# A transformer layer in float32r: weight chunks that begin at an offset of their own in each large product

## The chip, the cores and the metric

The kernel runs on one core of one Trainium2 chip. The metric is the device time of one execution in microseconds. TensorE (PE) multiplies, with its weight loads traced apart (PEld); VectorE (DVE) and ScalarE (ACT) do the elementwise work, GpSimd (POOL) and SyncE (SP) issue most transfers. SBUF, the on-chip memory, has 128 partitions; an address here is a byte within a partition, and "byte 96 of 128" means an address that leaves 96 when divided by 128.

## What is computed

One layer over 256 positions of width 2,048: a projection into two attention branches and their gates, the two attentions, a merge, an output projection, and a gated FFN with a short convolution (width 5,632). All weights are float32.

```python
h = rms_norm(x, norm_mix_pre)
c_q, c_kv, k_r, q_s, k_s, v_s, gates = split(h @ w_in)
...
merged = g[:, :, 0] * (o_a @ w_o_mla) + g[:, :, 1] * (o_b @ w_o_swa)
x = x + rms_norm(merged @ w_out, norm_mix_post)
h = rms_norm(x, norm_ffn_pre)
a, b = split(h @ ffn_w_up)
c = conv_b + sum(conv_w[j] * shifted(a, j) for j in range(3))
x = x + rms_norm((gelu(c) * b) @ ffn_w_down, norm_ffn_post)
```

## The kernel before

A float32 product is done as three float32r products. Each operand is split into a high part (its value rounded to float32r) and a low part (what is left), and `mm3` (lines 142 to 145) adds high x high, high x low and low x high into one PSUM accumulator. The activations are the stationary operand, 128 columns at a time, and lie split in SBUF slots (`ah`, `al`, `bh`, `bl`, and `gh`, `gl` for the FFN); the weights are the moving operand.

`wchunk` (lines 101 to 120) brings a chunk of weights: up to 1,024 float32 in each partition, as two row blocks of 512 columns or four of 256. The DMA lands it in a raw tile (3 buffers); ACT writes the high part `whi` by a casting copy (L118), DVE subtracts for the low part `wlo` (L119). The two go into the pool `ring`, which has 5 buffers of each. A chunk's buffers come free when the matmuls that read them are done, so the chain DMA, ACT, DVE, PE runs some chunks ahead of the matmuls.

`gemm` (lines 147 to 174) is one large product: all 16 to 24 row blocks of a weight matrix, 512 columns of it (320 or 256 in three cases), for both halves of the 256 positions. It calls `wchunk`, then `mm3` for each row block and half, so 96 to 144 matmuls. After each chunk `tick` runs what is due of the attention or the convolution, small matmuls and transposes that stand between those of the product. There are 58 calls of `gemm`. A few chunks aren't in the ring: the last `w_out` product has its first three, and the first FFN product its first four, in pools of their own (`own`). The projections inside the MLA attention call `wchunk` too, and there the chunk is in some matmuls the stationary operand (`qn`, `kn`, lines 610 to 612).

The order of work on the engines comes from the program's order and the tile framework's scheduler. Nothing in it depends on addresses.

Where things lie matters here. Two small tiles, `line_a` (96 bytes) and `line_b` (32 bytes), stand ahead of the activation slots. With them, the slots, the ring's `whi` and `wlo` and the attention's operands all begin at byte 96 of 128. The ring's chunks are 4,096 bytes, a row block of 512 columns 2,048 bytes and a stationary block 512, so in every matmul of a large product both operands begin at byte 96 of 128.

Of the kernel before, what the change touches and what calls it, by code (L numbers as in the profile page):

```python
# [12 lines left out]
F32R = mybir.dt.float32r  # L13
# [6 lines left out]
P = 128  # L20
# [21 lines left out]
def trunk_layer(ctx, tc, x, g_mix_pre, g_mix_post, g_ffn_pre, g_ffn_post, w_in, g_q, w_q, g_kv, w_kv,  # L42
# [13 lines left out]
    base = ctx.enter_context(tc.tile_pool(name="base", bufs=1))  # L56
    ring = ctx.enter_context(tc.tile_pool(name="ring", bufs=RING))

    def sb(pl, shape, name, dt=F32, tag=None, bufs=None):
        return pl.tile(shape, dt, name=name, tag=tag or name, **({"bufs": bufs} if bufs else {}))  # L60
# [10 lines left out]
    def warm_up(n):  # L71
        for i in range(n):
            tc.keep_in_program_order(pe.matmul(warm[:, 0:P], ident_b, ident_b, start=True, stop=True))

    warm_up(WARM[0])
    causal = sb(base, [P, P], "causal", BF16)
# [20 lines left out]


    cnt = [0]

    def wchunk(src, shape, own=None, rawp=None):
        i = cnt[0]
        cnt[0] += 1
        n = int(np.prod(shape))
        raw = rawp.tile([P, 1024], F32, name=f"raw{i}", tag="xraw") if rawp else \
            ring.tile([P, 1024], F32, name=f"raw{i}", tag="raw", bufs=RAW)
        dst = raw[:, :n]
        if len(shape) == 2:
            dst = dst.rearrange("p (a b) -> p a b", a=shape[0])
        elif len(shape) == 3:  # L110
            dst = dst.rearrange("p (a b c) -> p a b c", a=shape[0], b=shape[1])
        if len(shape) == 3:
            for k in range(shape[0]):
                nc.sync.dma_start(dst[:, k], src[:, k])
        else:
            nc.sync.dma_start(dst, src)
        hi, lo = ((own or ring).tile([P, 1024], F32R, name=f"w{part}{i}", tag="w" + part) for part in ("hi", "lo"))
        act.copy(hi[:, :n], raw[:, :n])  # L118
        vec.tensor_tensor(lo[:, :n], raw[:, :n], hi[:, :n].bitcast(F32), op=ALU.subtract)  # L119
        return hi, lo  # L120
# [8 lines left out]
    def tick():  # L129
        for f in steps.pop(now[0], ()):  # L130
            f()
        now[0] += 1
# [5 lines left out]
    def new_acc(tag):  # L138
        i = cnt[0]
        return [pacc.tile([P, 512], F32, name=f"acc{tag}_{i}_{t}", tag="acc") for t in range(NT)]  # L140

    def mm3(o, ah, al, bh, bl, start, stop):
        pe.matmul(o, ah, bh, start=start, stop=False)  # L143
        pe.matmul(o, ah, bl, start=False, stop=False)  # L144
        pe.matmul(o, al, bh, start=False, stop=stop)  # L145

    def gemm(xh, xl, w, k0, nk, c0, n, split=False, pre=None, extra=None):

        kc = 1024 // n if n in (256, 512) else 2
        acc = new_acc("g")  # L150
        todo = []
        cuts = [0, 1, 2] + list(range(4, nk + 1, 2)) if pre else list(range(0, nk, kc)) + [nk]
        for ci, (k, ke) in enumerate(zip(cuts[:-1], cuts[1:])):
            kk = ke - k
            src = w[(k0 + k) * P:(k0 + k + kk) * P, c0:c0 + n].rearrange("(a p) n -> p a n", p=P)
            if pre and ci == 0:
                pre(k, ke)
            hi, lo = wchunk(src, [kk, n], *(extra or {}).get(ci, ()))
            if pre and ke < nk:
                pre(ke, cuts[ci + 2])  # L160
            for j in range(kk):
                kt = k + j
                wh, wl = hi[:, j * n:(j + 1) * n], lo[:, j * n:(j + 1) * n]
                for t in range(NT):
                    def go(kt=kt, t=t, wh=wh, wl=wl):
                        mm3(acc[t][:, :n], xh(k0 + kt)[:, t * P:(t + 1) * P],
                            xl(k0 + kt)[:, t * P:(t + 1) * P], wh, wl, kt == 0, kt == nk - 1)
                    if split and t == 1:
                        todo.append(go)
                    else:  # L170
                        go()
            tick()
        return acc, todo
# [59 lines left out]
    def columns(dst, rows, n):  # L233
        pg = pss.tile([P, 512], F32, name=f"pg{rows.tensor.name}", tag="s")
        ins = pe.transpose(pg[:, 0:n], rows[0:n, :], ident[0:n, 0:n])
        tc.keep_in_program_order(ins)
        vec.tensor_copy(dst, pg[:, 0:n])
# [52 lines left out]
    with tc.manual_schedule(engines={mybir.EngineType.DVE, mybir.EngineType.Activation, mybir.EngineType.SP}):  # L290
        columns(gmat[:, 0:16], grow, 16)
        warm_up(WARM[1])
        acc, _ = gemm(XH, XL, w_in, 0, KT, C_KS, 512, pre=x_cols)
        x_square(3)
# [156 lines left out]
    for g in range(4):  # L451
        acc, _ = gemm(XH, XL, w_in, 0, KT, C_QS + 512 * g, 512)
        swa_q(g, acc)
        b = now[0]
        for i in range(4):
            at(b + 1 + i // 2, lambda u=4 * g + i: swa_qT(u))
            swa_unit(4 * g + i, b + 2 + 2 * i)
# [33 lines left out]
    def rope(dst, src, tmp, t, which, nh):  # L491
# [7 lines left out]
        vec.tensor_tensor(dst, dst, tmp, op=ALU.add)  # L499

    acc, _ = gemm(XH, XL, w_in, 0, KT, 0, 512)
    nrm, tr = latent(acc, QR, 32, cqh, cql, "cq")
    nrm()
# [55 lines left out]
    def q_rope4(f, t0):  # L559
# [3 lines left out]
        def mms(t):  # L563
            if t == 0:
                st["w"] = wchunk(wq3[:, :, 4 * f:4 * f + 4, 128:192], [4, 4, 64])
                st["pt"] = pst.tile([P, 512], F32, name=f"qr{f}", tag="t")
            hi, lo = st["w"]
            for k in range(4):
                mm3(st["pt"][:, t * 256:(t + 1) * 256], CQH(k)[:, t * P:(t + 1) * P], CQL(k)[:, t * P:(t + 1) * P],
                    hi[:, k * 256:(k + 1) * 256], lo[:, k * 256:(k + 1) * 256], k == 0, k == 3)  # L570
# [23 lines left out]
    def mla_unit(u, t0):  # L594
# [4 lines left out]
        def proj(kind, name, wsrc, shape, nk, ch, cl, col, scale):  # L599
            def go(i):  # L600
                if i == 0:
                    if wsrc is not None:
                        st["w" + kind] = wchunk(wsrc, shape)
                    st["ps" + kind] = pst.tile([P, 512], F32, name=f"{name}{u}", tag="t")
                hi, lo = st["w" + kind]
                o = st["ps" + kind][:, i * 256:(i + 1) * 256]
                for k in range(nk):
                    c = col(k, i)
                    wh, wl = hi[:, c:c + P], lo[:, c:c + P]
                    pe.matmul(o, wh, ch(k), start=k == 0, stop=False)  # L610
                    pe.matmul(o, wh, cl(k), start=False, stop=False)  # L611
                    pe.matmul(o, wl, ch(k), start=False, stop=k == nk - 1)  # L612
                if i == 1:
                    hl = sb(p2, [P, 2, 512], f"{name}{u}", F32R, tag=name, bufs=2)
                    split_to(hl[:, 0, :], hl[:, 1, :], st["ps" + kind], scale)
                    st[kind] = hl
            return go
# [324 lines left out]


RING = 5
WARM = (12, 15)
EXTRA = 3
RAW = 3
# [48 lines left out]
```

## Time and profile before

| | us |
|---|---|
| median of 2 runs | 1,505.91 (1,505.42 to 1,506.39) |
| profiled execution | 1,506.43 |
| its span, first to last instruction | 1,504.7 |
| TensorE matmuls, busy | 1,487.0 |
| weight loads, busy | 1,247.7 |
| DVE, busy | 940.4 |
| ACT, busy | 801.1 |

Matmuls overlap in the pipeline, so their busy time and their single durations (about 390 ns for 512 columns) don't add up to the span. The distance between the starts of two matmuls in sequence is what one costs; the timeline, which lists each with its start to 0.01 us, shows it.

### The profile page before, as it was taken

The numbers are of one execution on the slowest core, as the hardware profiler recorded it, in microseconds if no ns is written. First come the engines' busy times: TensorE is split into PE (matmuls) and PEld (weight loads), VectorE is DVE, ScalarE is ACT, GpSimd is POOL, SyncE is SP. The second block draws the span as 40 slices with busy tenths as digits, with TensorE's granted clock in tenths as the row PEclk, the third lists the DMA queues.
The fourth block names the chain that finished last, engine by engine and source line by source line (L and its number), as shares of the span: only waits on it lengthen the run. The fifth ranks groups of instructions, "written<-read, shape, count | busy, mean of one in ns | idle before, by whom it ended". The sixth has DMA issues, their size and how long they took to land.

```text
span 1504.7 us, 20149 instructions
## 1 busy us (share of the span) xinstructions
PE 1487.0 (99%) x7347; PEld 1247.7 (83%) x7347; DVE 940.4 (62%) x1607; ACT 801.1 (53%) x1289; POOL 66.8 (4%) x114
## 2 busy tenths in 40 slices
PE   9999999999999999999999999999999999999997
PEld 6888888888899987888888888888888888888887
DVE  5688884444667764555676666666544466666755
ACT  6588874434555553444565555555443455555542
POOL 2122210000000002000000000000000000000000
PEclk9999999999999999999999999999999999999999
DMA  7776656666655558766656666666566666665563
GB/s 231 223 177 166 165 171 195 205 206 209 182 156 164 163 163 289 246 218 195 196 179 178 198 187 183 183 184 190 186 195 195 195 181 182 186 193 183 182 195 113
DMA packets 160803, 285.46 MB, mean 190 GB/s; under 512 B 18419, under 2 KB 33893, under 8 KB 160448
## 3 DMA queue, kind: packets, MB, share of 16 engines
q1 hardware_dynamic: 154736, 264.81, 57.6%
q0 software_dynamic: 5968, 19.36, 5.2%
q8 instruction: 58, 0.95, 0.3%
q14 instruction: 41, 0.34, 0.1%
HBM read 277.79 MB, written 6.34 MB: 189 GB/s over the span
## 4 chain that ended last, share of the span: by engine, by line
PE 91%; DVE 3%; DMA 3%; ACT 2%; issue 1%; SPq 0%; DVEq 0%; ACTq 0%
PE accg L145 27%; PE accg L144 27%; PE accg L143 27%; DMA raw<-in_w_in_dram 2%; PE fT L840 1%; DVE wlo L119 1%; DMA raw<-in_w_o_mla_dram 1%; ACT whi L118 1%; PE mpo L681 1%; ACT p L407 1%; PE ms L647 1%; PE qn L610 1%; PE qn L612 1%; PE qn L611 1%; PE ms L652 0%
## 5 line engine op out<-in xcount | busy, mean ns | idle before, releaser
L119 DVE TENSOR_TENSOR wlo<-raw,whi 128x1024 fp32r<-128x1024 f32 (+2 forms) x501 | 608.9, 1217 | 488.1 <-ACT whi L118 487.1
L118 ACT CAST whi<-raw 128x1024 fp32r<-128x1024 f32 (+2 forms) x501 | 523.1, 1045 | 593.3 <-PE accg L145 512.1
L143 PE MATMUL accg<-whi,bh 128*128 128x512 f32 x960 | 378.4, 394 | 0.0
L145 PE MATMUL accg<-whi,bl 128*128 128x512 f32 x960 | 374.8, 390 | 0.0
L144 PE MATMUL accg<-wlo,bh 128*128 128x512 f32 x960 | 374.3, 390 | 0.0
L143 PE MATMUL accg<-whi,ah 128*128 128x512 f32 (+2 forms) x896 | 344.7, 385 | 0.0
L144 PE MATMUL accg<-wlo,ah 128*128 128x512 f32 (+2 forms) x896 | 341.6, 381 | 0.5 <-DVE wlo L119 0.5
L145 PE MATMUL accg<-whi,al 128*128 128x512 f32 (+2 forms) x896 | 341.0, 381 | 0.0
L145 PEld LDWEIGHTS accg<-whi,bl 128*128 128x128 f32 x960 | 180.4, 188 | 38.2
L144 PEld LDWEIGHTS accg<-wlo,bh 128*128 128x128 f32 x960 | 180.7, 188 | 36.4
L143 PEld LDWEIGHTS accg<-whi,bh 128*128 128x128 f32 x960 | 180.6, 188 | 36.2
L145 PEld LDWEIGHTS accg<-whi,al 128*128 128x128 f32 x896 | 168.5, 188 | 31.6
L144 PEld LDWEIGHTS accg<-wlo,ah 128*128 128x128 f32 x896 | 168.8, 188 | 30.8 <-DVE wlo L119 1.6
L143 PEld LDWEIGHTS accg<-whi,ah 128*128 128x128 f32 x896 | 168.7, 189 | 29.3 <-ACT whi L118 0.6
L143 PE MATMUL accg<-whi,gh 128*128 128x512 f32 (+1 forms) x104 | 39.3, 378 | 0.0
L144 PE MATMUL accg<-wlo,gh 128*128 128x512 f32 (+1 forms) x104 | 38.8, 373 | 0.0
L145 PE MATMUL accg<-whi,gl 128*128 128x512 f32 (+1 forms) x104 | 38.3, 373 | 0.0
L407 ACT ACTIVATE p<-p,nm 128x128 f32<-128x128 f32 x64 | 28.3, 445 | 5.9 <-DVE nm L398 5.9
L840 PEld LDWEIGHTS fT<-ident,f 128*128 128x128 f32 x176 | 21.8, 140 | 5.7
L840 PE MATMUL fT<-ident,f 128*128 128x128 f32 x176 | 26.3, 272 | 0.0
L844 ACT ACTIVATE cc<-fT,cvT 128x256 f32<-128x256 f32 x44 | 24.3, 551 | 0.0
L143 PEld LDWEIGHTS accg<-whi,gh 128*128 128x128 f32 x104 | 19.6, 188 | 4.2 <-ACT gh L200 0.9
(304 smaller groups left out, 1286.9 us busy)
## 6 DMA issues: line engine op xcount, KB each, us to landing
raw<-in_ffn_w_up_dram SPq DMA_DIRECT2D x176, 512.0 KB, 4.0
raw<-in_w_in_dram SPq DMA_DIRECT2D x111, 512.0 KB, 4.4
raw<-in_ffn_w_down_dram SPq DMA_DIRECT2D x88, 512.0 KB, 3.9
raw<-in_w_o_swa_dram SPq DMA_DIRECT2D x32, 512.0 KB, 4.3
raw<-in_w_o_mla_dram SPq DMA_DIRECT2D x32, 512.0 KB, 4.7
raw<-in_w_out_dram SPq DMA_DIRECT2D x32, 512.0 KB, 3.9
raw<-in_mla_w_q_up_dram SPq DMA_DIRECT2D x48, 128.0 KB, 2.8
bias<-strip POOLq DMA_DIRECT2D x16, 256.0 KB, 4.3
```

The lines of the kernel that those rows point to most:

```text
L118: act.copy(hi[:, :n], raw[:, :n])
L119: vec.tensor_tensor(lo[:, :n], raw[:, :n], hi[:, :n].bitcast(F32), op=ALU.subtract)
L143: pe.matmul(o, ah, bh, start=start, stop=False)
L144: pe.matmul(o, ah, bl, start=False, stop=False)
L145: pe.matmul(o, al, bh, start=False, stop=stop)
L407: act.activation(pb[:, i, a:b], pb[:, i, a:b], AF.Exp, bias=st["nm"][:, i, t:t + 1], accum_out=st["sm"][:, i, t:t + 1])
L610: pe.matmul(o, wh, ch(k), start=k == 0, stop=False)
L611: pe.matmul(o, wh, cl(k), start=False, stop=False)
L612: pe.matmul(o, wl, ch(k), start=False, stop=k == nk - 1)
L647: pe.matmul(o, w, v_, start=n == 0, stop=False)
L840: pe.transpose(pt[:, q * 256 + t * P:q * 256 + (t + 1) * P], sa[t][q][:, i * P:(i + 1) * P], ident)
L844: act.activation(cc, a, AF.Identity, scale=w2, bias=cb_)
```

## The change

The ring's `whi` and `wlo` tiles get 32 elements (128 bytes) more. A table `LINE` has fourteen offsets in elements; a counter goes up at the start of each `gemm`, and until the next one every ring chunk is written, and read, from that offset on. So the first product begins its chunks 2 elements (8 bytes) into the tile, the second 4, and so on to 28, then 1, 3, 0 and round again. In bytes the offsets are 8, 16, 24, 32, 40, 48, 56, 64, 80, 96, 112, 4, 12 and 0. Chunks in pools of their own stay at 0, and the chunks of the MLA projections have the offset of the product in which they fall. The raw tiles, the activation slots and the DMAs are the same, and so is the list of instructions of each engine and its order.

```diff
     cnt = [0]
+    group = [0]
 
     def wchunk(src, shape, own=None, rawp=None):
...
-        hi, lo = ((own or ring).tile([P, 1024], F32R, name=f"w{part}{i}", tag="w" + part) for part in ("hi", "lo"))
+        o = LINE[group[0] % len(LINE)] if not own else 0
+        hi, lo = ((own or ring).tile([P, 1024 + (0 if own else 32)], F32R, name=f"w{part}{i}", tag="w" + part)[:, o:o + 1024]
+                  for part in ("hi", "lo"))
         act.copy(hi[:, :n], raw[:, :n])
         vec.tensor_tensor(lo[:, :n], raw[:, :n], hi[:, :n].bitcast(F32), op=ALU.subtract)
...
         acc = new_acc("g")
+        group[0] += 1
         todo = []
...
 RING = 5
+LINE = (0, 2, 4, 6, 8, 10, 12, 14, 16, 20, 24, 28, 1, 3)
```

## The prediction

> **What bounds the kernel now.** I read the page first, then the groups of instructions with shapes kept apart, then the timeline of TensorE, for the distance from one matmul's start to the next. The page's parts 1, 2 and 4:
>
> ```profile
> PE 1487.0 (99%) x7347; PEld 1247.7 (83%) x7347; DVE 940.4 (62%) x1607; ACT 801.1 (53%) x1289; POOL 66.8 (4%) x114
> PEclk9999999999999999999999999999999999999999
> PE 91%; DVE 3%; DMA 3%; ACT 2%; issue 1%; SPq 0%; DVEq 0%; ACTq 0%
> ```
>
> TensorE is busy throughout at the full granted clock, and 91% of the chain that ended last is its work. The groups (busy time, mean of one, idle time before):
>
> ```profile
> L119 DVE TENSOR_TENSOR wlo<-raw,whi 128x1024 fp32r<-128x1024 f32 x491 | 601.0, 1225 | 486.5 <-ACT whi L118 485.5
> L118 ACT CAST whi<-raw 128x1024 fp32r<-128x1024 f32 x491 | 516.0, 1052 | 591.0 <-PE accg L145 511.5 <-DMA raw<-in_w_o_mla_dram 24.4 <-issue 12.9
> L143 PE MATMUL accg<-whi,bh 128*128 128x512 f32 x960 | 378.4, 394 | 0.0
> L143 PE MATMUL accg<-whi,ah 128*128 128x512 f32 x800 | 316.5, 396 | 0.0
> L143 PE MATMUL accg<-whi,gh 128*128 128x512 f32 x88 | 34.7, 395 | 0.0
> ```
>
> Each group stands for three, since lines 143, 144 and 145 run equally often: 3 x (960 + 800 + 88) = 5,544 matmuls of 512 columns. Their 390 ns overlap and say little; the distance between starts is the price of one. In a product that nothing interrupts, first and last row of 105 in sequence (start, duration, instruction):
>
> ```profile
> 231.20 0.39 PE L143 MATMUL accg<-whi,ah 128*128 128x512 f32 x1
> ...
> 254.78 0.39 PE L145 MATMUL accg<-whi,al 128*128 128x512 f32 x1
> ```
>
> (254.78 - 231.20) / 104 = 0.2267 us, or 5,544 x 0.2267 = 1,257 us of the 1,504.7 us span. So a change of 1 ns in this distance is worth up to 5.5 us; everything hangs on it. What is it made of? Two shorter shapes, 320 columns (seven distances) and 256 columns (twelve, the last row ending the run):
>
> ```profile
> 204.34 0.31 PE L143 MATMUL accg<-whi,ah 128*128 128x320 f32 x1
> ...
> 205.36 0.31 PE L144 MATMUL accg<-wlo,ah 128*128 128x320 f32 x1
> ```
>
> ```profile
> 400.15 0.28 PE L610 MATMUL kn<-ckh,whi 128*128 128x256 f32 x1
> ...
> 401.59 0.39 PE L143 MATMUL accg<-whi,ah 128*128 128x512 f32 x1
> ```
>
> 1.02 / 7 = 0.146 us and 1.44 / 12 = 0.120 us. From 256 to 512 columns the distance grows by 106.7 ns, 0.417 ns a column; 512 columns are then 213.3 ns, and a remainder of 13.3 ns is left. It is there at 320 columns (133.3 + 13) and at 256 (106.7 + 13.3) too, so it belongs to the matmul, not to its columns. The remainder is what an operand's address could change.
>
> It isn't constant, though. After four transposes of another product's columns, in a stretch of the FFN:
>
> ```profile
> 809.07 0.48 PE L143 MATMUL accg<-whi,bh 128*128 128x512 f32 x1
> 809.38 0.40 PE L144 MATMUL accg<-wlo,bh 128*128 128x512 f32 x1
> 809.62 0.40 PE L145 MATMUL accg<-whi,bl 128*128 128x512 f32 x1
> ...
> 811.24 0.39 PE L143 MATMUL accg<-whi,bh 128*128 128x512 f32 x1
> 811.46 0.39 PE L144 MATMUL accg<-wlo,bh 128*128 128x512 f32 x1
> ...
> 814.41 0.39 PE L145 MATMUL accg<-whi,bl 128*128 128x512 f32 x1
> ```
>
> The nine distances from 809.38 to 811.46 take 2.08 us, 231.1 ns each, between 0.22 and 0.24 us apiece with no semaphore among them; the next thirteen take 2.95 us, 226.9 ns. So the reading of weights and of moving columns runs unevenly after a break and then settles at 226.7 ns, the same in every product. In the program before, both operands of these products begin at the same place within 128 bytes, byte 96, by the allocation described above. I take the settled state to be one of that pairing; nothing in this trace has the long shape in another, and that is the unknown.
>
> **The change, part by part.** The larger tiles: 5 buffers of two kinds, 128 bytes each, 1,280 bytes a partition. Everything allocated behind the ring moves by ten times 128 bytes and keeps its place within 128; the raw tiles, into which the DMAs write, stay where they were. I cost this at nothing; the transfers' cover, the DMA's 3% of the chain, is not touched. The instructions and their order on each engine are the same.
>
> The offset in the cast (L118) and the subtraction (L119): 1,024 elements at 1,052 and 1,225 ns, one element after the other. The trace has no such instruction at another start. Lower end nothing (the elements must still pass); upper end the longest single one of each line, as if all were such (shortest, median and longest in ns):
>
> ```profile
> L119 DVE TENSOR_TENSOR wlo<-raw,whi x501: 693/1225/1603, 7.9 to 1482.3; 128x1024 fp32r<-128x1024 f32 x164, 128x640 fp32r<-128x640 f32 x2, 128x512 fp32r<-128x512 f32 x1
> L118 ACT CAST whi<-raw x501: 608/1054/1109, 7.3 to 1481.2; 128x1024 fp32r<-128x1024 f32 x164, 128x640 fp32r<-128x640 f32 x2, 128x512 fp32r<-128x512 f32 x1
> ```
>
> That is 31% and 5% more. What hides it stands above: ACT waited 511.5 us for matmuls to free a buffer, DVE 485.5 us for ACT. Where that cover is gone, in the attention stretches at the start, these lines carry the chain for 1.1% and 0.8% of the span:
>
> ```profile
> by line: PE accg L145 27.0%; PE accg L144 27.0%; PE accg L143 27.0%; DMA raw<-in_w_in_dram 1.7%; PE fT L840 1.3%; DVE wlo L119 1.1%; issue 0.8%; DMA raw<-in_w_o_mla_dram 0.8%; ACT whi L118 0.8%; PE mpo L681 0.7%; ACT p L407 0.7%; PE ms L647
> ```
>
> That is 16.6 and 12.0 us, of which 31% and 5% are 5.7 us. I take 0, since nothing ties those longest ones to a start, and keep 5.7 as the upper end.
>
> The offset under the matmuls. The counter goes up before a product's first chunk, so of 58 products the 14th, 28th, 42nd and 56th begin at 0: 96 + 96 + 144 + 120 matmuls of 512 columns. The 36 that read the three spare chunks of the last w_out product stay too. 5,544 - 492 = 5,052 move. How many of those are settled now? The breaks, by rows:
>
> ```profile
> L840 PE MATMUL fT<-ident,f 128*128 128x128 f32 x176 | 26.3, 272 | 0.0
> L365 PE MATMUL pt<-ident,p 128*128 128x128 f32 x96 | 14.0, 275 | 0.2 <-ACT pth L200 0.2
> L365 PE MATMUL ptm<-ident,mp 128*128 128x128 f32 x48 | 6.5, 272 | 0.0
> L387 PE MATMUL s<-kx,x 128*128 128x256 f32 x64 | 12.3, 282 | 0.0
> ```
>
> 176 / 4 + 96 / 3 + 48 / 3 + 64 / 2 = 124 breaks with up to nine unsettled distances behind each, 1,116; some 3,940 are settled and moved. Bounds for one: the shortest single distance, 0.22 us, and the longest, 0.24 us, so about -4 and +10 ns beside 226.7 (the rows have steps of 10 ns). I take the mean of the unsettled nine, 231.1 ns, since it is what this trace shows whenever the two reads stand otherwise to each other: 3,940 x 4.4 ns = 17.3 us. With the 240 + 96 moved matmuls of 256 and 320 columns and the attention products that use ring chunks, well under a thousand at half of that, 1 us more.
>
> Sum: the profiled execution took 1,506.4 us (span 1,504.7 and 1.7 around it), 0.5 above the median of 1,505.9. 1,505.9 + 17.3 + 1 = 1,524 us.
>
> **The rivals.**
>
> *It settles all the same.* The settled state is reached from any start within nine matmuls; a start moved by a few bytes may be one more such start, and the loop finds its 226.7 ns again. Then 1,506, with up to 5.7 us of the cast and subtraction on top. For it: the remainder is the same for three shapes. And one group does have its moving operand elsewhere, at byte 32 of 128 with weights at 96:
>
> ```profile
> 409.91 0.28 PE L681 MATMUL mpo<-mpth,vh 128*128 128x256 f32 x1
> 410.03 0.28 PE L681 MATMUL mpo<-mptl,vh 128*128 128x256 f32 x1
> 410.14 0.22 PE L681 MATMUL mpo<-mpth,vh 128*128 128x128 f32 x1
> ```
>
> 0.12 and 0.11 us for 256 columns are no worse than 0.120. Against it: these come two at a time and never settle. The Trainium skill, page "SBUF — State Buffer", section "SBUF: two separate sides", has TensorE on ports of its own that wait for no other engine; by that alone the sum would be 1,506 as well. The trace agrees in that no engine's work shows in the distances; what TensorE's own two reads do to each other no row settles.
>
> *Faster.* The pairing of now, all starts at byte 96, could be the costly one, in which the weight read takes its 13.3 ns from the moving read each time, and another place sets it free. All of it gone: 5,052 x 13.3 ns = 67 us, 1,439; half gone, 1,472. It decides from 30.1 / 5,052 = 6.0 ns a matmul. Against it: over the nine unsettled distances, which pass through several pairings, the mean is above the settled one, and no single one is below 0.22.
>
> *Far slower.* Six of the fourteen offsets (1, 2, 3, 6, 10 and 14 elements) aren't multiples of four elements; 456 + 432 + 420 + 384 + 384 + 288 = 2,364 matmuls. If a read that begins inside a 16-byte piece cost one column time for each of 128 pieces, 128 x 0.417 = 53 ns, it would be 126 us, 1,632; it decides from 30.1 / 2,364 = 12.7 ns each. No row speaks for it, nor any against. The Trainium skill, same page, section "Specifications (TRN2)", gives lines of 16 bytes with a penalty for each new one; read as a stream, such a start touches 129 lines in place of 128, which at four column times of 1.7 ns would be an estimated 3.9 us and 1,510. No run here shows which reading holds.
>
> **How the numbers follow.** Forecast 0.46, with a range of its own from 1,512 to 1,543 (the settled distance replaced by 228 to 236 ns); settles 0.28; far slower 0.17; faster 0.09. Two per cent, 30.1 us, is about what a measurement of this kernel can tell from no change. Above 1,536 lie about a quarter of the forecast, 0.11, and 0.15 of the far slower case: 0.26. Below 1,476 lie 0.05 of the faster case. Within: 0.69. The range of 1,500 to 1,560 leaves out 0.07 of the faster case below and 0.10 of the far slower one above.
>
> **What would show it.** In the profile after, the distance in an uninterrupted product: right if products at offsets other than 0 stand near 231 ns while the 14th and 28th keep 226.7; settled, if all stand at 226.7; wrong on the faster side if any offset shows 213 to 220 over a whole product; the far slower case, if those six offsets alone stand above 239. Lines 118 and 119 should keep 1,052 and 1,225 ns, and the granted clock its nines. The prediction fails if the distance depends on the offset alone in steps that the unsettled rows don't hold, or if DVE or ACT become what matmuls wait for.

## The result, and the profile after

| | before | changed |
|---|---|---|
| median, us | 1,505.91 | 1,530.12 (1,527.22 to 1,533.02) |
| ratio, 95% interval | | 1.0157 (1.0130 to 1.0183) |
| profiled execution, us | 1,506.43 | 1,533.02 |
| its span, us | 1,504.7 | 1,531.3 |

The kernel became slower by 24 us where 18 had been forecast. Measured once more beside the experiments, in more rounds, the ratio was 1.0163 (1.0147 to 1.0179). Parts 1, 2 and 4 of the page after:

```profile
PE 1512.1 (99%) x7347; PEld 1250.6 (82%) x7347; DVE 941.0 (61%) x1607; ACT 799.5 (52%) x1289; POOL 66.7 (4%) x114
PEclk9999999999999999999999999999999999999999
PE 92%; DMA 2%; ACT 2%; DVE 2%; issue 1%; SPq 0%; DVEq 0%; ACTq 0%
```

TensorE has 25 us more, DVE 0.6 more, ACT 1.6 and POOL 0.1 less. The granted clock shows the same nines; its mean was 0.997 before and is 0.996. In the groups with shapes kept apart the two lines that write at the offset have kept their durations, and DVE and ACT wait longer than before, not less:

```profile
L122 DVE TENSOR_TENSOR wlo<-raw,whi 128x1024 fp32r<-128x1024 f32 x491 | 601.4, 1226 | 510.7 <-ACT whi L121 510.3
L121 ACT CAST whi<-raw 128x1024 fp32r<-128x1024 f32 x491 | 514.5, 1049 | 617.3 <-PE accg L148 521.4 <-DMA raw<-in_w_o_mla_dram 19.2 <-issue 18.9
L146 PE MATMUL accg<-whi,bh 128*128 128x512 f32 x960 | 383.5, 399 | 0.0
```

The timeline of TensorE shows where the time is: first and last matmul of the 10th, 12th, 13th and 14th product, each of 96 matmuls and so 95 distances, none interrupted:

```profile
259.16 0.40 PE L146 MATMUL accg<-whi,bh 128*128 128x512 f32 x1
...
281.34 0.40 PE L148 MATMUL accg<-whi,bl 128*128 128x512 f32 x1
...
303.83 0.40 PE L146 MATMUL accg<-whi,bh 128*128 128x512 f32 x1
...
326.34 0.40 PE L148 MATMUL accg<-whi,bl 128*128 128x512 f32 x1
326.58 0.39 PE L146 MATMUL accg<-whi,ah 128*128 128x512 f32 x1
...
348.41 0.40 PE L148 MATMUL accg<-whi,al 128*128 128x512 f32 x1
348.64 0.40 PE L146 MATMUL accg<-whi,bh 128*128 128x512 f32 x1
...
370.57 0.39 PE L148 MATMUL accg<-whi,bl 128*128 128x512 f32 x1
```

At 96 bytes of offset 22.18 / 95 = 233.5 ns, at 4 bytes 22.51 / 95 = 236.9, at 12 bytes 21.83 / 95 = 229.8, and at offset 0 21.93 / 95 = 230.8. The 14th product before took 226.6 ns a matmul:

```profile
342.04 0.39 PE L143 MATMUL accg<-whi,bh 128*128 128x512 f32 x1
...
363.57 0.39 PE L145 MATMUL accg<-whi,bl 128*128 128x512 f32 x1
```

So no product is settled any more, the one at offset 0 included. Over all distances below 0.3 us from one matmul of 512 columns to the next (some 5,270 in each trace, from the timeline's starts) the mean went from 227.59 to 232.35 ns; taken for all 5,544 matmuls, 4.76 ns are 26.4 us of the 26.6 us by which the span grew.

### The profile page after: what moved, and what is told of

The parts are those of the page before. It is cut to its first block, busy times and chain, and to the rows that moved or that the text cites. A ratio compares the mean times of both kernels' runs of the same rounds, so it can differ in the third digit from the quotient of the medians.

```text
span 1531.3 us, 20149 instructions
## 1 busy us (share of the span) xinstructions
PE 1512.1 (99%) x7347; PEld 1250.6 (82%) x7347; DVE 941.0 (61%) x1607; ACT 799.5 (52%) x1289; POOL 66.7 (4%) x114
## 4 chain that ended last, share of the span: by engine, by line
PE 92%; DMA 2%; ACT 2%; DVE 2%; issue 1%; SPq 0%; DVEq 0%; ACTq 0%
PE accg L146 28%; PE accg L148 27%; PE accg L147 27%; DMA raw<-in_w_in_dram 2%; PE fT L844 1%; DMA raw<-in_w_o_mla_dram 1%; PE mpo L685 1%; PE ms L651 1%; DVE wlo L122 1%; ACT whi L121 1%; ACT p L411 1%; PE qn L615 0%; PE qn L614 0%; PE qn L616 0%; PE ms L656 0%
## 5 line engine op out<-in xcount | busy, mean ns | idle before, releaser
L146 PE MATMUL accg<-whi,bh 128*128 128x512 f32 x960 | 383.5, 399 | 0.0
L148 PE MATMUL accg<-whi,bl 128*128 128x512 f32 x960 | 379.3, 395 | 0.0
L147 PE MATMUL accg<-wlo,bh 128*128 128x512 f32 x960 | 378.8, 395 | 0.0
L146 PE MATMUL accg<-whi,ah 128*128 128x512 f32 (+2 forms) x896 | 348.4, 389 | 0.6 <-ACT whi L121 0.6
L147 PE MATMUL accg<-wlo,ah 128*128 128x512 f32 (+2 forms) x896 | 345.1, 385 | 0.5 <-DVE wlo L122 0.5
L844 PE MATMUL fT<-ident,f 128*128 128x128 f32 x176 | 26.4, 272 | 0.0
```

What stands on the lines that cost most here:

```text
L844: pe.transpose(pt[:, q * 256 + t * P:q * 256 + (t + 1) * P], sa[t][q][:, i * P:(i + 1) * P], ident)
```

## The experiments

The offset-0 products were the puzzle. In the changed kernel a buffer of the ring is 4,224 bytes, 33 x 128, so that buffers stand by turns at byte 224 and byte 96 of 256, while the weights that the matmul holds (the activation slots) all begin at byte 224 of 256. Before, every block stood at 224. Theory A: what counts is the place within 256 bytes of the moving block against the weights. Theory B: only the offset within 128 bytes counts, as the prediction had it.

**A control.** A padding of 256 bytes needs room, so one kernel has only the changes that make it.

```diff
-    relx = sb(lpool, [33, SH], "relx")
+    sb(p0, [P, 4352], "fill")
+    relx = sb(p0, [33, SH], "relx")
...
-    sel = sb(lpool, [33, 384], "sel")
+    sel = sb(p0, [33, 384], "sel")
...
-    first_extra[EXTRA + 2] = (None, p8)
```

> A control: the kernel before, with two small tiles of the start moved and one spare raw chunk of the first FFN product left to the ring, which makes the room that a larger padding needs. Both theories: ratio to the kernel before within 0.3% of 1, and the settled distance of 226.7 ns in every uninterrupted product.

Measured: 1.0012 (1.0003 to 1.0022). The room costs 0.1%.

**The padding alone**, the changed kernel without offsets.

```diff
-LINE = (0, 2, 4, 6, 8, 10, 12, 14, 16, 20, 24, 28, 1, 3)
+LINE = (0,)
```

> The 128 bytes more for each ring chunk, all offsets 0. Theory A (what counts is the place of the moving block against the weights being loaded, within 256 bytes; 128 bytes of padding puts every other buffer at the other half): products lose the settled 226.7 ns and stand near 230.5 as the offset-0 products of the changed kernel do, so about 5,544 x 3/4 x 3.8 = 16 us more, 1,522 us, ratio 1.010. Theory B (the offset within 128 bytes alone counts, the padding is free): 226.7 ns, ratio 1.000. That ACT, DVE or DMA is what got slower: no change of the distances either way, ratio 1.000 here.

Measured: 1,518.50 us, 1.0089 (1.0072 to 1.0106). The 14th product in its timeline:

```profile
344.86 0.39 PE L146 MATMUL accg<-whi,bh 128*128 128x512 f32 x1
...
366.88 0.39 PE L148 MATMUL accg<-whi,bl 128*128 128x512 f32 x1
```

22.02 / 95 = 231.8 ns, and 230.18 over the whole trace. Theory B falls: a padding with no offset at all costs 13 us.

**The ring moved as a whole**, by 128 bytes, against the kernel before. `line_d`, behind the ring, keeps what follows in its place.

```diff
     ring = ctx.enter_context(tc.tile_pool(name="ring", bufs=RING))
+    behind = ctx.enter_context(tc.tile_pool(name="behind", bufs=1))
...
+    sb(behind, [P, 32], "line_d")
...
     OH, OL = pair_view(oth), pair_view(otl)
+    sb(base, [P, 32], "line_c")
```

> No padding and no offset: the whole ring moved by 128 bytes against the activation slots, so that all blocks of a large product stand 128 bytes off within 256 and at the same byte of 128. Theory A: an even pairing other than the one before, 231 to 234 ns in every product, 5,544 x 3/4 x 4 to 7 = 17 to 29 us more, ratio 1.011 to 1.019. Theory B: 226.7 ns, ratio 1.000.

Measured: 1,530.18 us, 1.0165 (1.0149 to 1.0180), as slow as the changed kernel, with every buffer alike and every block at the same byte of 128 as before. The 14th product, with a few rows from its middle:

```profile
346.02 0.40 PE L145 MATMUL accg<-whi,bh 128*128 128x512 f32 x1
...
355.09 0.39 PE L145 MATMUL accg<-whi,bh 128*128 128x512 f32 x1
355.32 0.39 PE L146 MATMUL accg<-wlo,bh 128*128 128x512 f32 x1
355.55 0.39 PE L147 MATMUL accg<-whi,bl 128*128 128x512 f32 x1
...
356.01 0.40 PE L146 MATMUL accg<-wlo,bh 128*128 128x512 f32 x1
356.25 0.40 PE L147 MATMUL accg<-whi,bl 128*128 128x512 f32 x1
...
368.10 0.39 PE L147 MATMUL accg<-whi,bl 128*128 128x512 f32 x1
```

22.08 / 95 = 232.4 ns. The distances don't become one number, they go on changing between about 0.23 and 0.24 us: the unevenness that lasted nine matmuls before lasts here for the whole product.

**Everything moved together** by 32 bytes, slots, ring and all behind, so that blocks begin at byte 0 of 256.

```diff
-    sb(base, [P, 24], "line_a")
+    sb(base, [P, 32], "line_a")
```

> No padding and no offset: slots, ring and all that is behind moved together by 32 bytes, so that blocks begin at byte 0 of 256, and the pairing stays. Theory A in the form that the place of the two against each other counts: 226.7 ns and a ratio of 1.000. In the form that the place of the moving block by itself counts: as offset 32, 233.3 ns, 5,544 x 3/4 x 6.6 = 27 us more, ratio 1.018; and a start at byte 0 could then also be a faster one, down to 213 ns.

Measured: 1,504.64 us, 0.9997 (0.9987 to 1.0007).

```profile
340.88 0.39 PE L143 MATMUL accg<-whi,bh 128*128 128x512 f32 x1
...
362.41 0.39 PE L145 MATMUL accg<-whi,bl 128*128 128x512 f32 x1
```

21.53 / 95 = 226.6 ns. So in this move it is the two operands' place against each other that counts, not the place of either.

**Padding of 256 bytes**, in the changed kernel with the control's changes, first with all offsets 0, then with the offsets of the change.

```diff
-        hi, lo = ((own or ring).tile([P, 1024 + (0 if own else 32)], F32R, name=f"w{part}{i}", tag="w" + part)[:, o:o + 1024]
+        hi, lo = ((own or ring).tile([P, 1024 + (0 if own else 64)], F32R, name=f"w{part}{i}", tag="w" + part)[:, o:o + 1024]
...
-LINE = (0, 2, 4, 6, 8, 10, 12, 14, 16, 20, 24, 28, 1, 3)
+LINE = (0,)
```

> 256 bytes of padding (with the control's changes to make room) and all offsets 0. Theory A: nothing is lost, 226.7 ns in every uninterrupted product, ratio to the kernel before as the control's, 1.001. If larger chunks cost something by themselves: 1.005 or more.

Measured: 1.0021 (1.0011 to 1.0031), against 1.0012 of the control; the two intervals overlap. Settled again:

```profile
346.71 0.39 PE L146 MATMUL accg<-whi,bh 128*128 128x512 f32 x1
...
368.25 0.39 PE L148 MATMUL accg<-whi,bl 128*128 128x512 f32 x1
```

21.54 / 95 = 226.7 ns. A padding that keeps the place within 256 bytes costs nothing that can be told from the control. With `LINE` as in the change:

> 256 bytes of padding in place of 128 (with the control's changes to make room), and the offsets of the changed kernel, so that a product's blocks all stand alike within 256 bytes. Theory A: the products at offset 0 settle at 226.7 ns again, those at other offsets have each one even distance of their own; if half of the loss was the padding's, ratio 1.008, and if the offsets cost the same without it, 1.015. Theory B: the same as the changed kernel, ratio 1.016, product by product; the offset-0 products at 226.7.

Measured: 1,529.33 us, 1.0157 (1.0142 to 1.0172). The 12th and the 14th product:

```profile
301.31 0.40 PE L146 MATMUL accg<-whi,bh 128*128 128x512 f32 x1
...
323.90 0.40 PE L148 MATMUL accg<-whi,bl 128*128 128x512 f32 x1
...
346.13 0.39 PE L146 MATMUL accg<-whi,bh 128*128 128x512 f32 x1
...
367.68 0.39 PE L148 MATMUL accg<-whi,bl 128*128 128x512 f32 x1
```

237.8 ns at 4 bytes, 226.8 at offset 0, where the changed kernel had 230.8. So the offsets cost about as much without the padding's part as with it: padding alone 13 us, offsets alone 24 (22 over the control), both 24 to 25. The two don't add up. One reading is that a matmul that has lost its settled state can't lose it twice; no run here tests it. Means of all distances at each offset, in ns, in this kernel and in the changed one:

| bytes | 0 | 4 | 8 | 12 | 16 | 24 | 32 | 40 | 48 | 56 | 64 | 80 | 96 | 112 |
|---|---|---|---|---|---|---|---|---|---|---|---|---|---|---|
| 256 padded | 227.1 | 237.8 | 234.4 | 229.2 | 231.7 | 233.5 | 233.3 | 233.5 | 232.7 | 232.3 | 228.9 | 231.1 | 233.3 | 231.1 |
| the change | 229.9 | 236.8 | 233.6 | 230.1 | 231.2 | 233.4 | 232.9 | 233.1 | 231.8 | 232.0 | 231.4 | 231.8 | 233.4 | 231.6 |

**The other places within 256 bytes**, with the same padding.

```diff
-LINE = (0, 2, 4, 6, 8, 10, 12, 14, 16, 20, 24, 28, 1, 3)
+LINE = (0, 63, 62, 61, 60, 58, 56, 54, 52, 50, 48, 46, 44, 40, 36, 34, 33, 30, 26, 22, 18, 17, 5, 7)
```

> 256 bytes of padding again, with 24 offsets, among them the rest of the 256 bytes that the changed kernel did not visit (28, 68, 72, 88, 104, 120, 132 to 252 bytes). Theory A: each offset has a distance of its own, the same wherever it comes up, most between 229 and 238 ns; offset 0 at 226.7. If 0 is the best of all places, none falls below 226.7; if the pairing of before is only a good one, some offset stands at 224 or less over a whole product. As a whole some 1,525 us.

Measured: 1,539.03 us, 1.0223 (1.0203 to 1.0244), 14 us more than expected. No offset has a mean below 226.7. Next to 0 (228.1 here, since both of its products are interrupted) come 28 bytes with 227.4 and 252 with 228.5; the others stand between 231.7 and 238.5. A product at 68 bytes:

```profile
1203.98 0.40 PE L146 MATMUL accg<-whi,bh 128*128 128x512 f32 x1
...
1226.78 0.40 PE L148 MATMUL accg<-whi,bl 128*128 128x512 f32 x1
```

22.80 / 95 = 240.0 ns: it has settled, but with a remainder of 26.7 ns over the 213.3 of its columns, twice that of before.

**One operand of three out of place.** First the low slots of the activations, the weights of line 145, by 128 bytes:

```diff
     xth = [slot_a(p, "h") for p in range(8)]
+    sb(base, [P, 32], "line_e")
     xtl = [slot_a(p, "l") for p in range(8)]
+    sb(base, [P, 32], "line_f")
...
     oth = [slot_b(p, "h") for p in range(8)]
+    sb(base, [P, 32], "line_g")
     otl = [slot_b(p, "l") for p in range(8)]
+    sb(base, [P, 32], "line_h")
```

> No padding and no offset: only the low slots of the activations (the weights of the third matmul of each three) moved by 128 bytes. If the moving block meets the weights that are loaded during it, those of the next matmul, the distance behind line 144 is the long one (about 234 ns), behind 143 and 145 it is 226 to 227. If it is the weights of the matmul itself, the one behind line 145 is. Either way one in three is longer by about 7 ns: 5,544 / 3 x 3/4 x 7 = 10 us, ratio 1.006, unless the three no longer settle at all, then 1.01 to 1.016.

Measured: 1,523.26 us, 1.0119 (1.0104 to 1.0134). First row, some of the middle and last row of the 14th product:

```profile
346.53 0.39 PE L143 MATMUL accg<-whi,bh 128*128 128x512 f32 x1
...
354.85 0.39 PE L143 MATMUL accg<-whi,bh 128*128 128x512 f32 x1
355.07 0.40 PE L144 MATMUL accg<-wlo,bh 128*128 128x512 f32 x1
355.31 0.40 PE L145 MATMUL accg<-whi,bl 128*128 128x512 f32 x1
355.54 0.39 PE L143 MATMUL accg<-whi,bh 128*128 128x512 f32 x1
...
368.48 0.40 PE L145 MATMUL accg<-whi,bl 128*128 128x512 f32 x1
```

21.95 / 95 = 231.1 ns, 3 x (231.1 - 226.7) = 13.2 ns more for each three, and the rows have it behind lines 144 and 145 both: over the product the means behind lines 143, 144 and 145 are 226.7, 232.3 and 234.3 ns. Neither of the two readings in the expectation holds alone. Then the ring's low chunks instead, the moving block of line 144 (149 in this kernel); `line_d` stands behind the ring as before:

```diff
-        hi, lo = ((own or ring).tile([P, 1024], F32R, name=f"w{part}{i}", tag="w" + part) for part in ("hi", "lo"))
+        hi = (own or ring).tile([P, 1024], F32R, name=f"whi{i}", tag="whi")
+        if i == 0:
+            ring.tile([P, 32], F32, name="line_w", tag="line_w", bufs=1)
+        lo = (own or ring).tile([P, 1024], F32R, name=f"wlo{i}", tag="wlo")
```

> No offset: only the ring's low chunks (the moving block of line 144's matmul, here line 149) moved by 128 bytes, the weights all in place. Moving the low weights by 128 bytes made two of three distances long. If a matmul's moving block meets only what is loaded while it runs, here one of three is long: 226.7, 234 and 226 behind the three lines (148, 149, 150), as in the chunks of the changed kernel that had this pairing; 5,544 / 3 x 3/4 x 7 = 10 us more, ratio 1.006. If a block off its place disturbs its neighbours as well, two of three are long and the ratio is 1.012.

Measured: 1,525.12 us, 1.0135 (1.0118 to 1.0152), which is the ratio of the second reading; the distances hold to neither throughout. The 14th product, the 43rd of 144 matmuls, and the 29th and the 31st (this one from its second matmul, since transposes stand just ahead of it):

```profile
344.85 0.40 PE L148 MATMUL accg<-whi,bh 128*128 128x512 f32 x1
...
366.80 0.39 PE L150 MATMUL accg<-whi,bl 128*128 128x512 f32 x1
...
1136.98 0.39 PE L148 MATMUL accg<-whi,ah 128*128 128x512 f32 x1
...
1169.72 0.39 PE L150 MATMUL accg<-whi,gl 128*128 128x512 f32 x1
...
780.96 0.39 PE L148 MATMUL accg<-whi,bh 128*128 128x512 f32 x1
...
802.71 0.39 PE L150 MATMUL accg<-whi,bl 128*128 128x512 f32 x1
...
827.23 0.40 PE L149 MATMUL accg<-wlo,bh 128*128 128x512 f32 x1
...
849.17 0.39 PE L150 MATMUL accg<-whi,bl 128*128 128x512 f32 x1
```

21.95 / 95 = 231.1 and 32.74 / 143 = 229.0 ns; 21.75 / 95 = 228.9 and 21.94 / 94 = 233.4 ns. Behind lines 148, 149 and 150 stand 230.7, 229.7 and 233.0 ns in the 14th product, 226.7, 234.2 and 225.7 in the 43rd, which is the first reading, and 236, 234 and 230 in the 31st. The places within 256 bytes are the same in all four products, in the 29th and the 31st the very same slots are the weights, and the means are not the same.

**A version that might beat both.** In the kernel before, the operands of the MLA projections stand 128 bytes off the ring's chunks. One small tile at the head of their pool puts them at the same byte of 256.

```diff
     esl, lpool = open_pool("lpool")
+    sb(lpool, [P, 32], "line_l")
```

> The kernel before with the operands of the MLA projections (lines 610 to 612, and 143 to 145 under v and qr) moved by 128 bytes, so that they stand at the same byte of 256 as the ring's chunks; before they stand 128 off. 480 matmuls of 256 columns. Theory A: if 256 columns are hurt as 512 are, by 5 to 7 ns at most, 480 x 6 = 3 us less, ratio 0.998. If so short a matmul is bound by its weight load anyway (120 ns then and now): 1.000.

Measured: 1,505.03 us, 0.9993 (0.9982 to 1.0003): no gain that can be told from none. No kernel measured here is faster than the one before by more than the noise.

**The change again**, for its ratio beside the others:

> The changed kernel once more, beside the others on one chip. Theory A: ratio 1.013 to 1.018, product by product the same distances as in its first profile.

Measured: 1,531.21 us, 1.0163 (1.0147 to 1.0179); the mean over all distances is 232.39 ns, 232.35 in its first profile.

## Why the prediction was right, and where not

*What bounds the kernel* held: 4.76 ns more a matmul is 26.4 us of the 26.6.

*The mechanism* held as far as it went: the settled 226.7 ns belongs to one pairing of the two operands' places, and most other pairings stay uneven (68 bytes settle, at 240.0). What carried the forecast was the row that showed the uneven state inside the kernel before. Moving both operands (0.9997) and moving one of them (1.0165) show that it is their pairing.

*The larger tiles* were costed at nothing because everything keeps its place within 128 bytes. This step failed. The place that counts is the one within 256, and the padding alone costs 13 us. It is also why the 14th, 28th, 42nd and 56th products, which were left out of the 5,052, lost their settled state with the rest. The prediction's sign that they would keep 226.7 ns came out false. In the total this error hardly shows, since the offsets alone cost about as much as offsets and padding together; that is luck.

*The price*: 4.4 ns for 3,940 matmuls was 17.3 us; the trace has 26.4. The mean of the nine unsettled distances, 231.1, was what the mildest offsets have, but 4 bytes stand at 236.8 and most at 231.6 to 233.6; and of the 492 matmuls left out the 456 in products at offset 0 lost 229.9 - 226.9 = 3.0 ns each through the padding (226.9 is the mean of the same products before). The bounds of 0.22 and 0.24 us held the means. The 1 us for the shorter matmuls came out at nothing: the two last products, of 256 columns, took 14.31 and 14.01 us from first to last start, before 14.27 and 14.28.

*The cast and the subtraction* cost nothing, as taken: 1,049 and 1,226 ns against 1,052 and 1,225.

*It settles all the same* fell with the first trace. The page "SBUF — State Buffer" of the Trainium skill (section "SBUF: two separate sides") is about what other engines do to TensorE. The trace agrees with it there: the 10th, 11th and 12th product before keep 226.7 ns while DVE is busy for 9.8 to 10.8 us of each one's 21.5 and ACT for 8.7 to 9.2. That the places of TensorE's own two operands change the distance, the run with the ring moved shows (232.4 ns).

*Faster* fell: of 37 places in the two kernels with 256 bytes of padding none had a mean below 226.7 ns for matmuls of 512 columns.

*Far slower* fell: the six offsets inside a 16-byte piece have a mean of 233.2 ns in the changed kernel, the seven others 232.0. The 1.2 ns between them is no more than the prediction's estimate of 1.7 by the 16-byte lines of the Trainium skill (page "SBUF — State Buffer", section "Specifications (TRN2)"), and it isn't one rule for the six: 12 bytes has 230.1, 4 bytes 236.8.

What stays open is how the two reads meet. The low weights out of place lengthened two of three distances; the low chunks out of place lengthened one or all three, by the product, and the same places gave 228.9 and 233.4 ns in the 29th and the 31st, so what came before a matmul plays a part too. No run here shows the hardware's own reason for 256 bytes.

## What to carry to other kernels

Where TensorE is busy throughout, take the distance between the starts of two matmuls, not their durations, and look whether it is one number or wanders; a wandering one can be a matter of addresses. For float32r matmuls of 512 columns like these, keep the moving block and the weights at the same byte of 256, which also means that a padding of chunks should be a multiple of 256 bytes. A stretch in which a kernel briefly runs in another state gives a first price for an edit that may put it there for good (231.1 ns here, against a mean of 232.35 in the changed kernel).

## What had not been expected

That the distance settles at more than one value: 226.7 ns and, at 68 bytes, 240.0, which are 13.3 and 26.7 ns over the columns. That for 512 columns the best of the places tried is the plain one, both operands alike, and that its neighbours at 4 and 248 bytes, with 237.8 and 231.7, are not good ones, while 252 is.

That 256 columns don't follow this. The 58th product, of 120 such matmuls, in the kernel before, with both operands alike, and in the one with 256 bytes of padding and the offsets of the change, where its blocks stand 16 bytes off the weights:

```profile
1481.02 0.28 PE L143 MATMUL accg<-whi,ah 128*128 128x256 f32 x1
...
1495.30 0.28 PE L145 MATMUL accg<-whi,gl 128*128 128x256 f32 x1
```

```profile
1501.53 0.28 PE L146 MATMUL accg<-whi,ah 128*128 128x256 f32 x1
...
1515.42 0.28 PE L148 MATMUL accg<-whi,gl 128*128 128x256 f32 x1
```

14.28 / 119 = 120.0 ns and 13.89 / 119 = 116.7 ns: out of place is faster here. With the ring moved by 128 bytes the same product has 118.7. So the remainder of 13.3 ns that the prediction found at this length is no floor. For 240 matmuls it is under 1 us, too little to see in the times.
